# Branch B of a hybrid encoder layer by seven half products, with operand sums held in DRAM

## The chip, the core and the metric

The kernel runs on one core of one Trainium2 chip. The metric is device microseconds of one execution. Three runs of the kernel before gave 1960.22, 1960.53 and 1967.05 us; the median is 1960.53 us.

## The reference

One layer over 2048 tokens of width 1024: a projection to 7168 columns, banded attention (branch A), retention (branch B), both gated and projected, merged, projected again, normalised. What the change touches is the end of it: the gated output of branch B times `w_out_ret`, the merge, and the product with `w_out`.

```python
o_r = retention_chunkwise(qr, kr, v_r.reshape(B, S, R_HEADS, R_VAL_DIM), gn_gain[l])
branch_r = jnp.einsum('bsf,fd->bsd', o_r * jax.nn.silu(g_r), w_out_ret[l])

mixed = jax.nn.sigmoid(m_a) * branch_a + jax.nn.sigmoid(m_r) * branch_r
x = x + jnp.einsum('bsd,de->bse', mixed, w_out[l]).astype(x.dtype)
return rms_norm(x, final_gain)
```

## The kernel before, in words

Everything is float32. Each operand of a large product is split into a high and a low fp32r part, and a product of 128 x 128 weights with 128 x 512 data takes three matmuls: high by high, high by low, low by high. The fixed operand of a stage lies in seven resident pairs of tiles `R[0..6]`, each 128 x 4 x 512; the other operand streams through as chunks of 256 columns, each of them two raw tiles of 512 KB.

A stage is a `Job`. The projections (`p0`, `g0`, `p1`, `g1`) and the last stage (`out`) use the class `Strassen`: a chunk is 2 x 2 halves and is done with seven half products in place of eight, each of 12 matmuls. That needs sums of halves on both sides: `t1` to `t4` of the streaming side are made on POOL (`sum`), and the sums of the resident side stand in `R`. Five PSUM tiles (x, y, v, z, w) are combined by DVE and ACT (`product`).

The output products of branch A (`ba0`, `ba1`) and of branch B (`br0`, `br1`) use the class `Plain`: halves without sums. `ba` has 4 chunks of 4 half products in each half of the tokens, `br` 4 chunks of 8. The number behind a name is the half of the tokens (1024 each). For `br0` and `br1` the eight quarter operands are gated rows: `finish_yr` loads the retention output, its gate and the norm factor (three tiles of 256 KB), multiplies on DVE and POOL and splits into `R`, or, for the first eight, stores to `yrscr` during `p1`, whence `fill_yr` fetches them. `w_out` is loaded and summed during `br1` (`fill_wo`) and split into `R` at its end (`place_wo`).

What sets the order: the program is written by hand. `step()` emits one step of PE work, three matmuls, and then whatever `later(n, ...)` has put n steps ahead. Weights are made three products ahead (`AHEAD`), the high part by ACT (`make`), the low part by DVE four steps later. The engines take this order as written, except that before the change `strict[0]` is off from the opening of the last phase (`mrg`) until the last chunk of `br1`, where a scheduler may reorder ACT, DVE and POOL. Transfers go through SP's queue in the written order; raw chunks of `Strassen` stages go through ACT's queue. Gates (`ga`, `gr`) and earlier results (`ta`) are loaded ahead of each epilogue, and its result is stored (`tas`, `mxs`). SP stops at a store until its data is there.

`p1` starts with two chunks that alternate, product by product (`front=2`, orders `first` and `second`): each pair of `R` is then used twice before the next is needed, while `reload` refills `R`. `out` before starts with one chunk in a special order `s`.

## Time and profile before

| what | us |
|---|---|
| median of three runs | 1960.53 |
| profiled execution, span | 1957.6 |
| PE busy, of the span | 1904.1 (97%) |
| DVE, POOL, ACT busy | 1393.9, 982.5, 936.0 |
| first matmul of `p1`, of its third chunk | 767.46, 810.53 |
| first matmul of `ba0` | 1522.77 |
| first matmul of `br0`, of `out` | 1614.34, 1788.94 |
| last matmul of `out` begins | 1947.44 |

Of the profiled execution the page gives the span; the median of the runs is 2.9 us above it. PE is busy nearly throughout, so the table is read by stages: how many matmuls a stage issues, and how much longer it takes than they need.

### The profile page before, as it was taken

Reading aid. Unit: us, or ns where it says so; the run is one execution under the profiler, and the core shown is the slowest. Engines: PE = TensorE matmul, PEld = TensorE weight load, DVE = VectorE, ACT = ScalarE, POOL = GpSimd, SP = SyncE. Lnnn points to the kernel's source line nnn. Section 1 sums busy time; section 2 is a strip of 40 time slices with the busy share of each in tenths; the row PEclk is TensorE's granted clock in tenths of the full one; section 3 lists DMA queues with packets and bytes.
Section 4 is the critical chain, followed back from the end, with each engine's and each line's share of the span. In section 5 each row is a group of like instructions: output and inputs, shape, how many; then the busy total and the mean of one; then the engine's idle time right before and its main releaser. Section 6 shows DMA issues by size and latency. Waiting matters only on the chain. (4 is left out here: it accounts for less than half of the span.)

```text
span 1957.6 us, 30307 instructions
## 1 busy us (share of the span) xinstructions
PE 1904.1 (97%) x9640; PEld 1589.9 (81%) x9640; DVE 1393.9 (71%) x2551; ACT 936.0 (48%) x1889; POOL 982.5 (50%) x795
## 2 busy tenths in 40 slices
PE   7999999999999999999999999999999999999997
PEld 6887778888888887778787888888888878887886
DVE  6977877677756668888887677765566755547876
ACT  7554564566654555443333555554455321223554
POOL 0543544455546675544544454454666114557775
PEclk9999999999999999999999999999999999999999
DMA  6576786756549987676675645553999899987674
GB/s 191 167 251 205 231 283 206 200 166 178 160 137 278 280 255 266 189 246 188 203 247 170 200 145 163 168 152 116 277 277 297 304 371 330 319 266 234 205 226 140
DMA packets 335054, 434.84 MB, mean 222 GB/s; under 512 B 30040, under 2 KB 194544, under 8 KB 334896
## 3 DMA queue, kind: packets, MB, share of 16 engines
q1 hardware_dynamic: 269152, 368.42, 59.2%
q10 hardware_dynamic: 65744, 64.50, 10.8%
q8 instruction: 77, 1.26, 0.3%
q14 instruction: 81, 0.66, 0.1%
HBM read 288.21 MB, written 144.60 MB: 221 GB/s over the span
## 5 line engine op out<-in xcount | busy, mean ns | idle before, releaser
L142 POOL TENSOR_SCALAR pr<-pr,rsum 128x640 f32<-128x640 f32 (+4 forms) x128 | 96.0, 750 | 226.3 <-DVE ptl L142 108.3
L142 POOL TENSOR_TENSOR t_p<-raw_p,t_p 128x512 f32<-128x512 f32 x50 | 74.0, 1480 | 142.9 <-DVE wl_p L142 129.1
L142 PE MATMUL ps_g_z<-r,wh_g 128*128 128x512 f32 x448 | 143.3, 401 | 2.2 <-DVE c_g L142 2.2
L142 DVE CUSTOM_DVE_ANT_0 pr<-wide,bt 128x640 f32<-128x640 f32 (+4 forms) x128 | 94.3, 737 | 71.6 <-PE wide L142 62.9
L142 PE MATMUL ps_g_x<-r,wh_g 128*128 128x512 f32 x448 | 143.0, 400 | 0.7 <-ACT u_g L142 0.7
L142 ACT ACTIVATE pr<-pr,mn 128x640 f32<-128x640 f32 (+4 forms) x128 | 98.0, 765 | 84.8 <-DVE mn L142 84.8
L142 PE MATMUL ps_p_z<-r,wh_p 128*128 128x512 f32 x416 | 131.5, 397 | 3.1 <-DVE c_p L142 3.1
L142 PE MATMUL ps_p_x<-r,wh_p 128*128 128x512 f32 x416 | 130.1, 394 | 1.5 <-ACT u_p L142 1.5
L142 DVE TENSOR_TENSOR ptl<-tp,pth 128x384 fp32r<-128x384 f32 x168 | 95.9, 573 | 40.7 <-ACT pth L142 40.3
L142 ACT CAST pth<-tp 128x384 fp32r<-128x384 f32 x168 | 84.6, 515 | 70.5 <-PE tp L142 66.7
L142 POOL TENSOR_TENSOR sl<-sm,sh 128x512 fp32r<-128x512 f32 x64 | 88.6, 1384 | 53.9 <-ACT sh L142 26.0
L142 DVE TENSOR_TENSOR wl_p<-t_p,wh_p 128x512 fp32r<-128x512 f32 x104 | 96.8, 932 | 2.1 <-ACT wh_p L142 2.1
L142 DVE TENSOR_TENSOR sm<-sr,dm 128x512 f32<-128x512 f32 x64 | 44.1, 688 | 75.2 <-PE sr L142 37.4
L142 PE MATMUL wide<-ka,qa 128*128 128x512 f32 (+2 forms) x448 | 94.7, 327 | 2.1 <-DVE mn L142 2.1
L142 POOL TENSOR_TENSOR wl_g<-t_g,wh_g 128x512 fp32r<-128x512 f32 x56 | 75.2, 1342 | 41.4 <-ACT wh_g L142 40.2
L142 PEld LDWEIGHTS tp<-ident,pr 128*128 128x128 f32 x560 | 71.3, 141 | 27.4 <-POOL pr L142 2.2
L142 PE MATMUL po<-pth,va 128*128 128x256 f32 x336 | 92.9, 297 | 0.0
L142 PE MATMUL tp<-ident,pr 128*128 128x128 f32 x560 | 89.0, 273 | 2.9 <-POOL pr L142 1.6
L142 PEld LDWEIGHTS wide<-ka,qa 128*128 128x128 f32 x448 | 75.5, 189 | 19.2 <-DVE mn L142 7.3
L142 PEld LDWEIGHTS ps_p_x<-r,wh_p 128*128 128x128 f32 x416 | 76.9, 188 | 17.5 <-ACT u_p L142 2.4
L142 PEld LDWEIGHTS ps_p_z<-r,wh_p 128*128 128x128 f32 x416 | 75.9, 188 | 18.3 <-issue 4.3
L142 PE MATMUL po<-ptl,va 128*128 128x256 f32 x336 | 88.4, 285 | 1.1 <-DVE ptl L142 0.2
(909 smaller groups left out, 6017.9 us busy)
## 6 DMA issues: line engine op xcount, KB each, us to landing
raw_g<-in_w_in_dram ACTq DMA_DIRECT2D x56, 512.0 KB, 5.3
raw_p<-in_w_in_dram ACTq DMA_DIRECT2D x50, 512.0 KB, 6.3
qa<-qas SPq DMA_DIRECT2D x128, 128.0 KB, 2.9
qr<-qrs SPq DMA_DIRECT2D x128, 128.0 KB, 4.3
vr<-vrs SPq DMA_DIRECT2D x64, 256.0 KB, 5.3
ka<-kas SPq DMA_DIRECT2D x40, 256.0 KB, 3.6
va<-vas SPq DMA_DIRECT2D x40, 256.0 KB, 3.1
kds<-kdt_k SPq DMA_DIRECT2D x32, 256.0 KB, 4.1
```

What stands on the lines that cost most here:

```text
L142: return tc.keep_in_program_order(op(*a, **k))
```

## The change

`br0` and `br1` become `Strassen` jobs: seven half products of 12 matmuls a chunk in place of eight. So all seven sums of the gated rows are needed. `piece_yr(s, k)` fetches four gated rows, multiplies them, makes the sums on POOL and DVE and stores seven tiles to `yscr`; it runs four times in `p1` for the first half of the tokens and four times from the opening of `mrg` for the second. `fill_yr` fetches the first half's 28 tiles during `ba0` and `ba1`; `reload` fetches the second half's 28 during the last chunk of `br0` and the first pair of `br1`. `piece_wo` does the same for `w_out` during `p1`, to `wscr`, and `reload` fetches it in the last chunk of `br1` and the first pair of `out`. The first two chunks of `br1` and of `out` alternate as in `p1`; the second chunk's raw quarters are loaded apart (`quarters`). Raw chunks of `br` go through ACT's queue instead of SP's. `strict[0]` stays on. Matmuls in the built program: 9624 before, 9528 now.

```diff
 ORDERS["f"] = LAST = (0, 3, 1, 2, 4, 5, 6)
-ORDERS["s"], ORDERS["o"], ORDERS["l"] = (0, 4, 3, 1, 2, 5, 6), (0, 4, 1, 2, 3, 5, 6), (0, 4, 1, 2, 5, 6, 3)
+ORDERS["b"] = ORDERS["g"]
+ORDERS["o"], ORDERS["l"] = (0, 4, 1, 2, 3, 5, 6), (0, 4, 1, 2, 5, 6, 3)
...
 TR_LATER = 16
-YR_0 = (2, 10, 1)
-YR_1 = (102, 15, 2)
+YR_0 = (12, 90)
+YR_1 = (6, 42)
+WO = (60, 90)
+PAIRED = ("p1", "br1", "out")
...
     orscr = [[D(f"ors_{p}_{b}", [2, P, B]) for b in range(NB)] for p in range(4)]
-    yrscr = [D(f"yrs_{h}", [P, B]) for h in range(HEADS)]
+    yscr = [[D(f"ys_{s}_{m}", [4, P, B]) for m in range(7)] for s in range(2)]
+    wscr = [D(f"ws_{m}", [4, P, B]) for m in range(7)]
...
             if name not in self.ps:
-                two_pools = self.job.name == "out" and name in ("z", "w")
+                two_pools = self.job.name in ("br0", "br1", "out") and name in ("z", "w")
...
         "second": {1: ("t1", "t2"), 2: ("t3",), 5: ("t4",)},
-        "s": {0: ("t1",), 3: ("t2",), 1: ("t3",), 2: ("t4",)},
+        "b": {0: ("t1", "t2"), 2: ("t3",), 6: ("t4",)},
...
             last = self.job.orders[self.c] == "l"
+            lags = (1, 14, 22, 30) if self.c < self.job.front else (1, 4, 7, 10)
             for k, q in enumerate(((1, 1), (1, 0), (0, 1), (0, 0)) if last else ((0, 0), (1, 1), (1, 0), (0, 1))):
-                later(1 + 3 * k, lambda q=q: load(q))
+                later(lags[k], lambda q=q: load(q))
...
             self.orders = [name[0]] * n
-            if name == "g0":
+            if name in ("g0", "br0", "br1"):
...
                 self.orders[front] = "h"
-            if name == "p1":
+            if name in PAIRED:
...
             if name == "out":
-                self.orders[0], self.orders[-1] = "s", "l"
+                self.orders[-1] = "l"
...
             if front:
-                seq[:0] = [(c, n) for n in LAST for c in range(front)] if name == "p1" else [
+                seq[:0] = [(c, n) for n in LAST for c in range(front)] if name in PAIRED else [
...
                 ]
-                if name == "p1":
+                if name in PAIRED:
...
+        for job in jobs:
+            if job.name in PAIRED:
+                one, two_, three = job.chunks[:3]
+                for ch in (one, two_, three):
+                    for lead in RAW_LEADS:
+                        sooner.pop(begins[ch] - lead)
+                two_.raw, three.raw = [], []
+                at = begins[one]
+                sooner[at - 9], sooner[at - 6] = (one, [0]), (one, [1])
...
         later(lag + 2, lambda: (low or dve).tensor_tensor(wl, r32(wl), r32(wh), ALU.subtract))
-    def reload(n):
+    def reload(n, src):
...
             t = 4 * at + k
-            later(1, lambda k=k, t=t: refill(m, k, cscr[m][k], 8 + 2 * t - 4 * at, pool if t % 3 == 2 else dve))
+            later(1, lambda k=k, t=t: refill(m, k, src[m][k], 8 + 2 * t - 4 * at, pool if t % 3 == 2 else dve))
...
+    def piece_yr(s, k):
+        tiles = {}
+        def fetch(i, j):
+            h, b = 4 * j + k, 2 * s + i
+            a, u, r = (E(f"{n}_{h}_{b}") for n in ("yr", "yv", "rb"))
+            tiles[i, j] = a
+            dma(a, orscr[h // 2][b][h % 2])
+            dma(u, urscr[h][b])
+            dma(r, rsscr[s][8 * b + h].rearrange("(o d) -> o d", o=1).broadcast_to([P, B]))
+            later(14, lambda: dve.scalar_tensor_tensor(a, a, gn[:, h:h + 1], u, ALU.mult, ALU.mult))
+            later(16, lambda: pool.tensor_tensor(a, a, r, ALU.mult))
+        def store(m, t, lag):
+            put(lag + 4, yscr[s][m][k], t)
+        def first():
+            s1 = tiles["s1"] = E(f"ys1_{s}_{k}")
+            pool.tensor_tensor(s1, tiles[1, 0], tiles[1, 1], ALU.add)
+            store(2, tiles[1, 1], 0)
+            store(3, s1, 3)
+        def second():
+            a11 = tiles[0, 0]
+            s2 = tiles["s2"] = E(f"ys2_{s}_{k}")
+            dve.tensor_tensor(s2, tiles["s1"], a11, ALU.subtract)
+            dve.tensor_tensor(tiles[1, 0], tiles[1, 0], a11, ALU.subtract)
+            store(0, a11, 0)
+            store(4, s2, 2)
+            store(5, tiles[1, 0], 2)
+        def third():
+            a12 = tiles[0, 1]
+            s4 = E(f"ys4_{s}_{k}")
+            pool.tensor_tensor(s4, a12, tiles["s2"], ALU.subtract)
+            store(1, a12, 0)
+            store(6, s4, 3)
+        for n, q in enumerate(((1, 0), (1, 1), (0, 0), (0, 1))):
+            later(1 + 3 * n, lambda q=q: fetch(*q))
+        later(23, first)
+        later(27, second)
+        later(30, third)
+    def fill_yr(n):
+        m = PRODUCTS[n][0]
         for k in range(4):
-            later(1 + 2 * k, lambda k=k: refill(m, k, yrscr[4 * j + k], 10))
+            later(1 + 2 * k, lambda k=k: refill(m, k, yscr[0][m][k], 10))
+    def quarters(ch, src):
+        ch.b = {}
+        for key in ("b11", "b12", "b21", "b22"):
+            ch.b[key] = E(f"{key}_{ch.job.name}", shape=(P, 4, P))
+            h = int(key[2]) - 1
+            dma(ch.b[key], src(int(key[1]) - 1)[:, :, h * P:(h + 1) * P])
...
             d, b = 2 * c + j, 2 * s + i
-            g, ta = C(f"gr_{d}_{b}"), C(f"ta_{d}_{b}")
+            g, ta = E(f"gr_{d}_{b}"), E(f"ta_{d}_{b}")
...
     def ep_br(s):
-        def epilogue(c, i, j, ps, got):
-            g, ta = got
-            dve.scalar_tensor_tensor(g, g, 1.0, ps, ALU.add, ALU.mult)
-            pool.tensor_tensor(g, g, ta, ALU.add)
+        def epilogue(c, i, j, src, ps):
+            g, ta = by_name[f"br{s}"].chunks[c].got.pop((i, j))
+            dve.scalar_tensor_tensor(g, g, 1.0, src, ALU.add, ALU.mult)
+            later(1, lambda: pool.tensor_tensor(g, g, ta, ALU.add))
...
         return epilogue
-    wo = {}
-    def fill_wo(k):
+    def piece_wo(k):
...
         s2, s3, s4 = (E(f"ws{n}_{k}") for n in (2, 3, 4))
-        wo[4, k], wo[5, k], wo[2, k], wo[6, k] = s2, s3, a[1, 1], s4
...
+        def store(lag, m, t):
+            put(lag, wscr[m][k], t)
...
             dve.tensor_tensor(s2, s3, a[1, 1], ALU.add)
+            pool.tensor_tensor(a[1, 0], a[1, 0], a[1, 1], ALU.add)
+            for n, (m, t) in enumerate(((0, a[0, 0]), (2, a[1, 1]), (5, s3), (4, s2), (3, a[1, 0]))):
+                store(2 + n, m, t)
...
+            store(5, 1, a[0, 1])
+            store(6, 6, s4)
...
     ]
-    RYA = [{(0, 0): 0, (1, 0): 4}, {(0, 0): 5, (1, 0): 2}]
-    RYR = [{(0, 0): 6, (0, 1): 1, (1, 0): 3, (1, 1): 0}, {(0, 0): 4, (0, 1): 5, (1, 0): 2, (1, 1): 6}]
+    RYA = [{(0, 0): 0, (1, 0): 4}, {(0, 0): 2, (1, 0): 6}]
...
         jobs.append(Job(f"br{s}", 4, w_stream(w_out_ret, [T * c for c in range(4)]), ep_br(s),
-                        resident=RYR[s], before=before_br(s)))
-    jobs.append(Job("out", 8, mx_stream, ep_out, (2, 5), before=before_out))
+                        before=before_br(s), front=2 * s))
+    jobs.append(Job("out", 8, mx_stream, ep_out, (2, 5), before=before_out, front=2))
+    by_name = {j.name: j for j in jobs}
...
     for n in range(7):
-        hook("g0", 13, n, lambda n=n: reload(n))
+        hook("g0", 13, n, lambda n=n: reload(n, cscr))
+        hook("br0", 3, n, lambda n=n: reload(n, yscr[1]))
+        hook("br1", 3, n, lambda n=n: reload(n, wscr))
...
     hook("g1", 13, 1, lambda: fill_ya(0, 1, 4))
-    for j in range(2):
-        hook("g1", 13, 6, lambda j=j: later(66 * j, lambda: fill_yr(j, RYR[0][0, j])))
...
         hook("ba0", 1 + i, 0, lambda i=i: fill_ya(1, i, RYA[1][i, 0]))
-    for k in range(4):
-        hook("br1", *divmod(1 + 6 * k, 8), lambda k=k: fill_wo(k))
-    hook("br1", 3, 2, lambda: strict.__setitem__(0, True))
-    for n, m in ((4, 4), (5, 5), (6, 2), (7, 6)):
-        hook("br1", 3, n, lambda n=n, m=m: place_wo(m, *((1, 1) if n < 6 else (n - 4, 2))))
+    for at, n in ((("ba0", 0, 1), 2), (("ba0", 2, 0), 3), (("ba0", 3, 0), 4), (("ba1", 0, 0), 0),
+                  (("ba1", 1, 0), 1), (("ba1", 3, 2), 5), (("ba1", 3, 3), 6)):
+        hook(*at, lambda n=n: fill_yr(n))
+    br1, out_job = by_name["br1"], by_name["out"]
+    hook("br0", 2, 4, lambda: quarters(br1.chunks[1], lambda j: br1.stream(1, j)))
+    hook("br1", 2, 4, lambda: quarters(out_job.chunks[1], lambda j: out_job.stream(1, j)))
...
     seq.extend((job, ch, n) for job in jobs for ch, n in job.seq)
-    for j in (jobs[0], jobs[2]):
-        for i in range(2):
-            hook(j.name, i, 1 if j is jobs[2] else (0, 1, 1), lambda j=j, i=i: j.chunks[2].load([i]))
+    for j in jobs:
+        for i in range(2 if j.front else 0):
+            hook(j.name, i, 1 if j.name in PAIRED else (0, 1, 1), lambda j=j, i=i: j.chunks[2].load([i]))
...
+    quarters(jobs[2].chunks[1], lambda j: jobs[2].stream(1, j))
     run_to(end["g0"])
-    for h in range(HEADS):
-        later(10 + 44 * h, lambda h=h: finish_yr(h, 0, None, 18))
+    for k in range(4):
+        later(YR_0[0] + YR_0[1] * k, lambda k=k: piece_yr(0, k))
+        later(WO[0] + WO[1] * k, lambda k=k: piece_wo(k))
...
     st.close()
-    strict[0] = False
     st = open_phase("mrg", E_MRG, 4)
-    free_at = end["br0"] - 12
...
+    for k in range(4):
+        later(YR_1[0] + YR_1[1] * k, lambda k=k: piece_yr(1, k))
...
```

SP's queue, where `ba1` ends and `br0` begins. `ga` and `gr` are gates on their way in, `ta` branch A's result, `tas` its store, `yr`, `yv`, `rb` the three inputs of a gated row, `r` a tile of `R`, `ys` the stored sums. Before:

```order
L142 DMA ga_7_2_18465<-mas_7_2_364 128x512
L142 DMA tas_6_2_424<-ga_6_2_18420 128x512
L142 DMA ga_7_3_18487<-mas_7_3_365 128x512
L142 DMA tas_6_3_425<-ga_6_3_18443 128x512
L142 DMA gr_0_0_18505<-mrs_0_0_366 128x512
L142 DMA ta_0_0_18506<-tas_0_0_398 128x512
L142 DMA tas_7_2_428<-ga_7_2_18465 128x512
```

Now, from the same load on:

```order
L145 DMA ga_7_2_18731<-mas_7_2_377 128x512
L145 DMA tas_6_2_437<-ga_6_2_18685 128x512
L145 DMA ga_7_3_18756<-mas_7_3_378 128x512
L145 DMA gr_0_0_18762<-mrs_0_0_379 128x512
L145 DMA ta_0_0_18763<-tas_0_0_411 128x512
L145 DMA yr_2_3_18769<-ors_1_3_317 128x512
L145 DMA yv_2_3_18770<-urs_2_3_289 128x512
L145 DMA rb_2_3_18771<-rss_1_453 128x512
L145 DMA tas_6_3_438<-ga_6_3_18709 128x512
L145 DMA gr_1_1_18784<-mrs_1_1_384 128x512
L145 DMA ta_1_1_18785<-tas_1_1_416 128x512
L145 DMA r21_86<-ys_0_2_328 128x512
```

Between the load of `ga_7_2` and the store of its product stood five transfers; now it is seventeen, of which the eleven rows under the first are shown.

ACT's queue, where `out` begins. `wh_out_c_n` is the high part of chunk c's weights for product n, `r40` the high part of `R[4]`, `ws2` a sum of `w_out` in SBUF, `r01` the raw tile that a refill has put in the low half. Before:

```order
L142 CAST r40_89<-ws2_0_19320 128x512
L142 CAST wh_out_0_0_19900<-raw_out_0_0_19804 128x512
L142 CAST r40_89<-ws2_1_19453 128x512
L142 CAST r40_89<-ws2_2_19586 128x512
L142 CAST r40_89<-ws2_3_19719 128x512
L142 CAST r50_91<-ws3_0_19321 128x512
L142 DMA raw_out_1_0_19928<-mxs_0_430 128x4x256
L142 CAST wh_out_0_4_19930<-t1_out_0_19865 128x512
```

Now:

```order
L145 CAST r00_81<-r01_82 128x512 x2
L145 CAST wh_out_0_0_20288<-raw_out_0_0_20122 128x512
L145 CAST r00_81<-r01_82 128x512
L145 CAST r10_83<-r11_84 128x512
L145 CAST wh_out_0_3_20317<-raw_out_0_1_20206 128x512
L145 CAST r10_83<-r11_84 128x512 x2
L145 CAST wh_out_1_0_20349<-b11_out_20112 128x512
L145 CAST r10_83<-r11_84 128x512
L145 CAST r40_89<-r41_90 128x512
L145 CAST wh_out_1_3_20377<-b21_out_20116 128x512
```

The weights of two chunks now come in turn, and every cast into `R` follows a transfer instead of a tile that lies in SBUF.

More of the change, by code (lines that the diff above doesn't have):

```diff
@@ L503, in dense @@
         sooner = {at - lead: (ch, [j]) for ch, at in begins.items() for j, lead in enumerate(RAW_LEADS)}
-        one, two_, three = jobs[2].chunks[:3]
-        for ch in (one, two_, three):
-            for lead in RAW_LEADS:
-                sooner.pop(begins[ch] - lead)
-        two_.raw, three.raw = [], []
-        at = begins[one]
-        sooner[at - 9], sooner[at - 6] = (one, [0]), (one, [1])
-        first_out = jobs[-1].chunks[0]
-        at = begins[first_out]
-        for lead in RAW_LEADS:
-            sooner.pop(at - lead)
-        sooner[at - 8], sooner[at - 5] = (first_out, [0]), (first_out, [1])
+        for job in jobs:
[7 more added lines that the diff above has]
+                sooner[at - 9], sooner[at - 6] = (one, [0]), (one, [1])
         operands = {begins[ch] - 2: ch for ch in begins if ch.job.before}
@@ L1101, in fill_ya @@
             later(1 + k, lambda k=k: refill(m, k, oascr[k][2 * s + i], 8))
-    def finish_yr(h, b, m, lead, hold=0):
-        a, u, r = (E(f"{n}_{h}_{b}") for n in ("yr", "yv", "rb"))
-        dma(a, orscr[h // 2][b][h % 2])
-        dma(u, urscr[h][b])
-        dma(r, rsscr[b // 2][8 * b + h].rearrange("(o d) -> o d", o=1).broadcast_to([P, B]))
-        def gated():
-            dve.scalar_tensor_tensor(a, a, gn[:, h:h + 1], u, ALU.mult, ALU.mult)
-        later(lead, gated)
-        later(lead + 2, lambda: pool.tensor_tensor(a, a, r, ALU.mult))
-        if m is None:
-            put(lead + 8, yrscr[h], a)
-            return
-        wh, wl = (w[:, h % 4, :] for w in R[m])
-        at = max(lead + 5, hold - steps[0])
-        later(at, lambda: act.copy(wh, a))
-        later(at + 2, lambda: dve.tensor_tensor(wl, a, r32(wh), ALU.subtract))
@@ L1819, in hybrid_kernel @@
     st.close()
-    strict[0] = False
     st = open_phase("mrg", E_MRG, 4)
-    free_at = end["br0"] - 12
-    for s, (first, every, of) in enumerate((YR_0, YR_1)):
-        for n, (i, h) in enumerate((i, h) for i in range(1 - s, 2) for h in range(HEADS)):
-            hold = free_at + h % 4 if s and i and h > 3 else 0
-            later(
-                first + every * n // of,
-                lambda s=s, i=i, h=h, hold=hold: finish_yr(h, 2 * s + i, RYR[s][i, h // 4], 8, hold),
-            )
+    for k in range(4):
+        later(YR_1[0] + YR_1[1] * k, lambda k=k: piece_yr(1, k))
     while step():
```

21 lines of the change are left out of this document (removed).

## The prediction

> **What bounds the kernel now.** The page's first line says that PE is busy almost throughout, so I read PE's own waits from branch A's output products to the end, then the stretches of that part, then the instants at which stages begin.
>
> ```profile
> PE 1904.1 (97%) x9640; PEld 1589.9 (81%) x9640; DVE 1393.9 (71%) x2551; ACT 936.0 (48%) x1889; POOL 982.5 (50%) x795
> PE ps_out_x L142 <- ACT u_out L142: 3.4, 1, 3.4
> PE ps_out_z L142 <- DVE c_out L142: 0.7, 1, 0.7
> ```
> ```profile
> core 0: us, PE busy (x) PEld busy (x) DVE busy (x) ACT busy (x) POOL busy (x), PEclk, DMA share, GB/s
> 1553.00:1614.30 61.30, 61.18 (x266) 49.32 (x265) 35.56 (x56) 14.78 (x25) 10.31 (x8) 1.00 1.00 363
> 1614.30:1701.40 87.10, 87.10 (x385) 72.11 (x385) 47.76 (x65) 18.51 (x33) 41.16 (x29) 1.00 0.96 332
> 1701.40:1788.90 87.50, 87.31 (x385) 72.03 (x384) 45.63 (x55) 20.46 (x37) 47.75 (x34) 1.00 0.76 251
> 1788.90:1814.40 25.50, 21.42 (x86) 16.69 (x86) 22.66 (x21) 11.03 (x23) 22.26 (x14) 0.93 0.76 244
> ```
>
> The second and third line are two of three waits of PE after 1523 us (the third is 0.2 us). In the table the first row is the end of branch A's products, the next two are `br0` and `br1`, the last is the first chunk of `out`. PE is the bound of branch B: no wait, full clock. Beside it the column before the last shows something nearly as full: the DMA engines, 1.00 and 0.96 of their time.
>
> **The change part by part.**
>
> ```profile
> 1614.34 0.61 PE L142 MATMUL ps_br_(0, 0)_18528<-r,wh_br_(0, 0)_18462 128*128 128x512 f32 x2
> 1788.94 0.61 PE L142 MATMUL ps_out_x<-r,wh_out 128*128 128x512 f32 x2
> 1814.39 0.62 PE L142 MATMUL ps_out_x<-r,wh_out 128*128 128x512 f32 x2
> 1833.43 0.62 PE L142 MATMUL ps_out_x<-r,wh_out 128*128 128x512 f32 x2
> ```
>
> *Products.* These rows open `br0`, `out`, and the second and third chunk of `out`. A chunk of seven products is 84 matmuls and takes 1833.43 - 1814.39 = 19.04 us without a wait, 0.2267 us each (2.72 us a product; a step of the program is three, 0.68 us). Branch B takes 1788.94 - 1614.34 = 174.6 us for 768 matmuls. 672 take 152.3 us: **-22.3 us**. Nothing hides this, since PE is the bound.
>
> *Start of `out`.* Its first chunk takes 1814.39 - 1788.94 = 25.45 us, 6.4 more than the next. `place_wo` then fills ACT and DVE with splits of `w_out`, and one wait does most of the harm:
>
> ```profile
> 1797.91 0.90 PE L142 MATMUL ps_out_x<-r,wh_out 128*128 128x512 f32 x2 [3.37 <-ACT u_out L142]
> 1798.00:1802.00 4.00, 4.00 (x11) 3.13 (x12) 4.00 (x4) 2.46 (x5) 4.00 (x4) 0.57 0.98 367
> ```
>
> PE waits 3.37 us for the copy of a product, and in the 4 us behind it the granted clock is 0.57. The alternating start replaces this chunk: **-6.4 us**, but it has a price of its own, which `p1` shows, since it starts in the same way.
>
> ```profile
> 767.46 0.61 PE L142 MATMUL ps_p_x<-r,wh_p 128*128 128x512 f32 x2
> 810.53 0.61 PE L142 MATMUL ps_p_x<-r,wh_p 128*128 128x512 f32 x2
> 767.50:810.50 43.00, 39.53 (x169) 31.12 (x168) 42.81 (x46) 24.19 (x46) 30.15 (x18) 1.00 0.65 226
> 810.50:1058.90 248.40, 243.91 (x1124) 200.04 (x1123) 204.66 (x276) 92.90 (x178) 110.65 (x75) 1.00 0.68 219
> 1059.51 0.71 PE L142 MATMUL ps_g_x<-r,wh_g 128*128 128x512 f32 x2
> ```
>
> The first two rows open `p1` and its third chunk, the last opens the stage behind `p1`.
>
> Two chunks take 810.53 - 767.46 = 43.07 us where 168 matmuls need 38.08: 5.0 us lost, with DVE busy 42.81 of 43.00. `br1` and `out` each do the same on DVE (28 refills, of which POOL takes nine, 14 low parts, the combinations of two chunks): twice 5.0, **+10.0 us**, between 4 (`br1` and `out` have two more PSUM tiles a chunk from the second pool) and 14.
>
> *More work in `p1`.* `piece_yr` and `piece_wo` bring 32 operations to DVE and 32 to POOL where `finish_yr` had eight and eight.
>
> ```profile
> L142 DVE SCALAR_TENSOR_TENSOR yr<-yr,gn,yv 128x512 f32<-128x512 f32 x7 | 5.2, 744 | 0.0
> L142 DVE TENSOR_TENSOR wl_p<-t_p,wh_p 128x512 fp32r<-128x512 f32 x48 | 45.6, 950 | 0.0
> L142 DVE TENSOR_TENSOR c_p<-ps_p_z,u_p 128x512 f32<-128x512 f32 x13 | 9.0, 690 | 0.4
> L142 POOL TENSOR_TENSOR t_p<-raw_p,t_p 128x512 f32<-128x512 f32 x23 | 33.5, 1457 | 70.8 <-DVE wl_p L142 62.1 <-DMA raw_p<-in_w_in_dram 6.4 <-POOL t_p L142 2.0
> L142 POOL TENSOR_TENSOR yr<-yr,rb 128x512 f32<-128x512 f32 x7 | 11.6, 1664 | 6.4 <-DVE yr L142 6.4
> ```
>
> 24 more at 0.744 to 0.950 us are 18 to 23 us of DVE, 24 at 1.457 to 1.664 are 35 to 40 us of POOL. In `p1` behind its first pair DVE is busy 204.66 of 248.40 us, so the work fits on average (some 90%), but DVE works in order and every low part of a weight passes through it. If a fifth of DVE's addition comes at a bad moment, **+4 us**; the bounds are 0 (all of it in DVE's idle time) and 10 (half of it on the path). The transfers, 88 more, take about 60 us of the DMA engines in 291 us, where the share is 0.65 to 0.68: covered.
>
> *Branch B's other engines.* POOL gets 32 sums, some 47 us at 1.457 us, in 152 us where it was busy 89 of 175 and loses half of the gated rows: it has room. DVE in `br0` gets 28 low parts (26.6 us), 20 combinations and 16 epilogues at 0.69 us (25 us), and about 22 us of refills and gated rows, 73 of 76 us. I cost this at nothing only because the next term makes PE wait at the same place; without that wait it may cost 0 to 5 us.
>
> *Transfers.* Here is the term that decides. In the trace the DMA engines are full for 30 us, at this rate and these landing times:
>
> ```profile
> DMA packets 7092, 11.64 MB, mean 388 GB/s; under 512 B 662, under 2 KB 2173, under 8 KB 7090
> ga<-mas SPq DMA_DIRECT2D x11, 256.0 KB, 5.3
> r<-yrs SPq DMA_DIRECT2D x4, 256.0 KB, 6.3
> out_dram<-fg SPq DMA_DIRECT2D x30, 256.0 KB, 2.2
> ```
>
> The first three lines are from 1560 to 1590 us, the last is the median of the stores in `out`, where little else moves. From 1553 us to the end of `br0` the kernel now moves 363 GB/s x 61.3 us + 332 x 87.1 = 51.2 MB in 148.4 us. In the built order the same stretch has 181 transfers before and 227 after: 21 loads of gated rows fewer, but 32 more fills of `R`, 28 stores of sums, and some single ones. 46 more of 0.262 MB make 63.3 MB. At 388 GB/s that is 163.1 us, and PE will need only 61.3 + 76.2 = 137.5 us: 25.6 us of transfers too many. Most come from the 20th us of the stretch on, when a piece's 12 loads and 7 stores join the gates and the fills.
>
> How much of it stays unnoticed? A gate of branch A is loaded two products (5.4 us) ahead of its epilogue, and the low parts that stand behind that epilogue on DVE are due eight steps (5.4 us) later. A fill's cast stands ten steps (6.8 us) behind its transfer, and the weights behind it on ACT are due 12 steps (8.2 us) later. Less the 2.2 us of an easy landing, a backlog of 8.7 to 12.8 us does no harm. So PE waits 12.8 to 16.9 us. I take the low end, **+13 us**, because the worst backlog stands where the fills for `br0` do. The bounds are 0 and the whole 25.6. That `br`'s raw chunks go through ACT's queue frees SP, not the engines: in the 30 us above SP's queue alone had them full.
>
> The Trainium skill, "DMA: Bandwidth & Descriptors", section Specifications, puts the limit of a core towards HBM at about 358 GB/s and that of the ports at 435. The trace's 388 lies between them and decides. By 358 the surplus would be an estimated 39 us and the change slower; by 435 it would be an estimated 8 us, within what does no harm, which is the first rival below.
>
> **Sum:** -22.3 - 6.4 + 10.0 + 4 + 13 = -1.7 us, a span of 1955.9. The median of the runs is 2.9 us over the profiled span (1960.53 to 1957.6), so **1958.8 us**: no change. What a measurement of this kernel can tell from no change is about 0.5%, 9.8 us: faster means below 1950.7, slower above 1970.3.
>
> **The rivals.**
>
> *The transfers hide.* If the backlog never exceeds what is tolerated (loads issued with their buffers free, stores that can wait, engines that move more than 388 GB/s when the mix has more stores), the 13 us go: -14.7 us, **1945.8**. For it: the existing queue is full for 60 us (share 1.00) and PE does not wait once. Against it: the surplus is twice the tolerated backlog.
>
> *SP's queue becomes the bound.* SP takes its transfers in order and stops at a store until its data is there. Seventeen transfers instead of five then lie between a gate and the store of its product, twelve more at 0.68 us each, 8 us. If a late gate stops the store, and the stop keeps loads back that would have filled the engines, nothing of the surplus is hidden. PE then waits 25.6 us in several pieces, some above the 3.37 us at which the granted clock fell to 0.57; three such pieces at 1.7 us (the 4 us at 0.57) add 5. With 7 us in `p1` the sum is -22.3 - 6.4 + 10 + 7 + 25.6 + 5 = +19, **1979**. It decides from about 21 us of waiting on, since -28.7 + 10 + 7 + 21.5 is the 9.8 of a slower kernel. The Trainium skill, "TensorE: Matmul & The Clock Gate", Part 1, has the clock fall after an idle window of about 3.4 us and return after as long a busy one; the trace agrees here (3.37 us), and by it waits well below cost no clock.
>
> *The change does not give what it says*: the sums cost PE elsewhere as much as the products gave, by DVE in `p1` and branch B (10 + 5 us) and both starts (14): -28.7 + 29, **1961** with the transfers hidden.
>
> **How the numbers follow.** The forecast has 0.42, the hidden transfers 0.32, SP's queue 0.23, the last 0.03. Faster by over 0.5% is the second case, 0.32; slower the third, 0.23; within 0.5% the first and last, 0.45. The range reaches to both rivals' times, 1942 to 1979: about half of the slow one lies above it and a quarter of the hidden one below (0.11 + 0.08). The likeliest case alone runs from 1952 to 1969 (DMA term from 8 to 20, `p1` and starts as bounded).
>
> **What the profile after would show.** 12 matmuls fewer per chunk of branch B: its first to last matmul without waits 152.3 us. The start of `out` to its third chunk 43 us, with waits for DVE. In the list of PE's waits from 1553 us to the end of `br0`: behind them ACT's casts into `R` and DVE's epilogues that wait for DMA, the DMA share at 1.0 for all of `br0`, landing times of gates and fills above 12 us. If these land in 6 us, the transfer term is wrong; if `p1` (292.1 us from 767.46 to 1059.51) grows by over 10 us, that term is; if PE waits for DVE alone, it is the third rival.

## The result, and the profile after

The changed kernel takes 2047.54 us (median of 4 runs, 2044.40 to 2051.89) against 1960.82 us of the kernel before (4 runs): a ratio of 1.0437, 95% interval 1.0419 to 1.0454. It is slower by 87 us, where no change was forecast.

The page, then the rows of PE that open `p1`, its third chunk, `g1`, `br0`, `br1`, `out` and `out`'s third and fourth chunk:

```profile
PE 1914.0 (94%) x9544; PEld 1581.6 (77%) x9544; DVE 1528.0 (75%) x2645; ACT 967.2 (47%) x1945; POOL 1087.8 (53%) x853
```
```profile
767.31 0.61 PE L145 MATMUL ps_p_x<-r,wh_p 128*128 128x512 f32 x2
...
820.08 0.39 PE L145 MATMUL ps_p_x<-r,wh_p 128*128 128x512 f32 x1
...
1092.97 0.48 PE L145 MATMUL ps_g_x<-r,wh_g 128*128 128x512 f32 x1
...
1676.96 0.39 PE L145 MATMUL ps_br_x<-r,wh_br 128*128 128x512 f32 x1
...
1775.84 0.39 PE L145 MATMUL ps_br_x<-r,wh_br 128*128 128x512 f32 x1
...
1866.31 0.39 PE L145 MATMUL ps_out_x<-r,wh_out 128*128 128x512 f32 x1
...
1917.67 0.39 PE L145 MATMUL ps_out_x<-r,wh_out 128*128 128x512 f32 x1
...
1939.67 0.39 PE L145 MATMUL ps_out_x<-r,wh_out 128*128 128x512 f32 x1
```

There are 96 matmuls fewer, and DVE is busy 134 us longer. From one opening to the next (the same rows taken in both traces, `ba0` opening at 1522.77 and 1557.91, and the experiments below read likewise):

| stage | before | after | change | of it products alone |
|---|---|---|---|---|
| p1, first two chunks (the pair) | 43.1 | 52.8 | +9.7 | 38.1 |
| p1, the rest | 249.0 | 272.9 | +23.9 | 228.5 |
| ba0 + ba1 | 91.6 | 119.0 | +27.5 | |
| br0 | 87.1 | 98.9 | +11.8 | 76.2 |
| br1 | 87.5 | 90.5 | +3.0 | 76.2 |
| out, first two chunks | 44.5 | 51.4 | +6.9 | 38.1 |
| out, the rest | 114.0 | 117.0 | +3.0 | |

`g1` with attention and retention in it grows by 1.6 us; together 87 us. Now each engine in these stages (the columns are those of the prediction's tables):

```profile
767.30:820.10 52.80, 43.95 (x170) 33.88 (x169) 52.52 (x53) 24.98 (x47) 39.44 (x24) 0.90 0.78 266
820.10:1093.00 272.90, 251.59 (x1130) 203.10 (x1128) 231.37 (x295) 93.04 (x177) 141.47 (x95) 0.98 0.81 268
1557.90:1610.50 52.60, 47.25 (x217) 38.33 (x215) 32.73 (x52) 16.87 (x31) 5.75 (x5) 0.99 0.96 326
1610.50:1677.00 66.50, 52.00 (x193) 39.82 (x194) 38.10 (x48) 13.17 (x23) 19.53 (x14) 0.85 0.92 323
1677.00:1775.80 98.80, 82.36 (x337) 64.82 (x336) 80.03 (x85) 26.64 (x47) 65.40 (x42) 0.95 0.97 327
1775.80:1866.30 90.50, 81.13 (x337) 63.37 (x336) 83.57 (x85) 34.83 (x63) 67.40 (x43) 0.98 0.79 276
1866.30:1917.70 51.40, 41.53 (x170) 32.10 (x169) 49.91 (x44) 21.80 (x44) 44.98 (x28) 0.97 0.68 234
```

Two things stand out at once. In `ba` and `br0` (rows three to five) the DMA engines are nearly full (share 0.92 to 0.97) at 323 to 327 GB/s, not 388. In both pairs DVE is full, and in `br1` nearly so; its 85 operations there take 83.57 us, almost 1 us each. Why is seen beside POOL, first DVE's rows of the timeline in `br1`, then POOL's:

```profile
1783.67 1.77 DVE L145 TENSOR_TENSOR wl_br<-b_br,wh_br 128x512 fp32r<-128x512 f32 x1
1785.36 1.77 DVE L145 TENSOR_TENSOR r<-r,r 128x512 fp32r<-128x512 f32 x1
1787.05 1.77 DVE L145 TENSOR_TENSOR wl_br<-b_br,wh_br 128x512 fp32r<-128x512 f32 x1
1788.75 1.75 DVE L145 TENSOR_TENSOR r<-r,r 128x512 fp32r<-128x512 f32 x1
1790.43 0.68 DVE L145 SCALAR_TENSOR_TENSOR gr<-gr,ps_br_x 128x512 f32<-128x512 f32 x1
```
```profile
1784.85 1.73 POOL L145 TENSOR_TENSOR t_br<-b_br,b_br 128x512 f32<-128x512 f32 x1
1786.66 1.62 POOL L145 TENSOR_TENSOR t_br<-b_br,t_br 128x512 f32<-128x512 f32 x1
1788.24 1.71 POOL L145 TENSOR_TENSOR r<-r,r 128x512 fp32r<-128x512 f32 x1
1789.92 1.73 POOL L145 TENSOR_TENSOR t_br<-raw_br,raw_br 128x512 f32<-128x512 f32 x1
```

The two engines go in step, one operation of each every 1.7 us, and the only short one of DVE's reads an operand from PSUM (`ps_br_x`). The experiments test what that means. In `ba` SP's waits show a third thing. Behind them stand the transfer of ACT that the longest of them was for, and SP's transfers just before and after that wait:

```profile
SPq L145 <- DMA raw_br<-in_w_out_ret_dram: 15.8, 3, 5.8
```
```profile
1637.23 0.38 ACTq L145 DMA_DIRECT2D raw_br<-in_w_out_ret_dram  x1
```
```profile
1639.03 0.32 SPq L145 DMA_DIRECT2D rb<-rss  x1
1645.16 0.32 SPq L145 DMA_DIRECT2D r<-ys  x1
```

The program gives each transfer the next of eight semaphores in turn and lets it wait until the transfer eight before it has landed, whichever engine issued that. ACT issued the weight chunk `raw_br` late, behind casts that waited for their data, and SP, with a fill of `R` ready to go, stood 5.8 us until it had landed.

The fourth is the granted clock (the column PEclk). It falls to half at twelve places between the openings of `p1` and of `out`'s third chunk, where the kernel before has one. Here is one of them in `br0`, with the matmuls of PE and the windows of the fall and of what follows:

```profile
1738.77 0.50 PE L145 MATMUL ps_br_x<-r,wl_br 128*128 128x512 f32 x1 [1.83 <-DVE wl_br L145]
...
1739.95 1.05 PE L145 MATMUL ps_br_x<-r,wh_br 128*128 128x512 f32 x2
```
```profile
1739.60:1743.00 3.40, 3.40 (x10) 2.62 (x9) 3.40 (x4) 0.00 (x0) 2.77 (x3) 0.50 0.93 246
1743.00:1746.40 3.40, 3.40 (x15) 2.50 (x14) 3.40 (x4) 1.76 (x3) 3.40 (x3) 1.00 1.06 405
```

A wait of 1.83 us comes before 3.4 us at half clock, in which PE does ten matmuls instead of 15 (two of them in 1.05 us, where 0.61 is usual). So a wait can cost more than its own length: in `p1` PE is idle 22 us more than before and its matmuls take some 10 us longer.

### The profile page after: what moved, and what is told of

Same layout as the page of the kernel before. It is cut to its first block, busy times and chain, and to the rows that moved or that the text cites. A ratio compares the mean times of both kernels' runs of the same rounds, so it can differ in the third digit from the quotient of the medians.

```text
span 2045.1 us, 30651 instructions
## 1 busy us (share of the span) xinstructions
PE 1914.0 (94%) x9544; PEld 1581.6 (77%) x9544; DVE 1528.0 (75%) x2645; ACT 967.2 (47%) x1945; POOL 1087.8 (53%) x853
## 4 chain that ended last, share of the span: by engine, by line
PE 33%; DMA 12%; DVE 12%; issue 6%; POOL 4%; ACT 1%; SPq 1%; POOLq 0%; DVEq 0%; ACTq 0%
PE ps_g_z L145 4%; PE ps_g_x L145 4%; PE o L145 2%; PE po L145 2%; PE ps_g_v L145 2%; PE ps_g_y L145 2%; PE ps_g_w L145 2%; DMA raw_br<-in_w_out_ret_dram 2%; PE wide L145 2%; DVE r L145 2%; DMA r<-ys 2%; DVE wl_p L145 1%; POOL fg L145 1%; DMA yv<-urs 1%; PE tp L145 1%
## 5 line engine op out<-in xcount | busy, mean ns | idle before, releaser
L145 DVE CUSTOM_DVE_ANT_0 pr<-wide,bt 128x640 f32<-128x640 f32 (+4 forms) x128 | 94.3, 737 | 71.5 <-PE wide L145 63.3
L145 DVE TENSOR_TENSOR r<-r,r 128x512 fp32r<-128x512 f32 x101 | 107.4, 1075 | 11.3 <-ACT r L145 11.3
L145 ACT CAST r<-r 128x512 fp32r<-128x512 f32 x128 | 76.1, 618 | 71.5 <-DMA r<-ys 52.6
L145 POOL TENSOR_TENSOR yr<-yr,rb 128x512 f32<-128x512 f32 x32 | 47.7, 1492 | 108.4 <-DVE yr L145 103.0
L145 DVE TENSOR_TENSOR sm<-sr,dm 128x512 f32<-128x512 f32 x64 | 44.1, 689 | 79.8 <-PE sr L145 38.1
L145 DVE TENSOR_TENSOR wl_p<-t_p,wh_p 128x512 fp32r<-128x512 f32 x104 | 101.3, 975 | 1.7 <-ACT wh_p L145 1.7
L145 ACT CAST wh_p<-t_p 128x512 fp32r<-128x512 f32 x104 | 64.4, 619 | 60.5 <-DVE wl_p L145 21.5
L145 PEld LDWEIGHTS tp<-ident,pr 128*128 128x128 f32 x560 | 71.3, 140 | 27.5 <-POOL pr L145 2.2
```

The costliest lines, as they stand in the source:

```text
L145: return tc.keep_in_program_order(op(*a, **k))
```

## The experiments

A stage that an experiment leaves alone differs from one profiled execution to the next: `p1` takes 322.6 to 328.7 us, `ba0` to `br0` 217.9 to 223.2, `br0` 98.5 to 104.0, `br1` 88.4 to 90.5, `out`'s pair 51.4 to 52.4. A stage's change counts only if it leaves that range. The changed kernel's ratio is 1.0437 (1.0419 to 1.0454) throughout. The intervals of e1, e3, e4, e5, e6, e9, e10 and e15 overlap with it, so what these show is read from their stages.

**What the seven products cost alone (e8).**

```diff
-        hook("br0", 3, n, lambda n=n: reload(n, yscr[1]))
-        hook("br1", 3, n, lambda n=n: reload(n, wscr))
...
-            dma(ta, tascr[d][b])
...
-            later(1, lambda: pool.tensor_tensor(g, g, ta, ALU.add))
...
-        later(YR_1[0] + YR_1[1] * k, lambda k=k: piece_yr(1, k))
```

> Branch B's seven products stay, but what goes with them in br0 and br1 is left out: batch 1's pieces, the refills of R in br0's and br1's last chunks, and branch A's term (its loads and additions), so the output is not the reference's. If the products are as cheap as counted and DVE, POOL and the transfers eat the gain: br0 76 to 82 us, br1 76 to 79, the pair of out 38 to 41, ba0+ba1 105 or less. Rival, something in the seven products themselves (PSUM banks, the order of the chunks) holds PE up: br0 and br1 stay above 85.

The windows of `ba0`, `ba1`, `br0`, `br1` and `out`'s pair:

```profile
1561.70:1609.20 47.50, 46.92 (x218) 38.54 (x217) 32.05 (x53) 19.85 (x36) 5.64 (x4) 1.00 0.91 310
1609.20:1652.80 43.60, 43.60 (x194) 35.96 (x193) 25.91 (x37) 11.56 (x21) 4.45 (x3) 1.00 0.96 336
1652.80:1730.30 77.50, 76.75 (x338) 62.94 (x337) 49.27 (x71) 24.07 (x41) 28.66 (x21) 1.00 0.59 199
1730.30:1809.30 79.00, 76.97 (x337) 62.79 (x336) 44.27 (x65) 19.39 (x32) 16.96 (x13) 1.00 0.50 166
1809.30:1849.40 40.10, 38.75 (x170) 31.41 (x170) 23.58 (x28) 13.35 (x28) 22.08 (x17) 1.00 0.59 180
```

Ratio 1.0061 (1.0037 to 1.0084), with `p1` as long as in the changed kernel. Nearly all as counted, and `ba` is back at 91.1 us although it still fills `R` from DRAM. What eats the gain is what goes with the products, not the products; which part of it, e8 can't say, since it leaves out pieces, refills and branch A's term together.

**POOL and DVE (e3, e4, e5).** e3 leaves POOL's additions of branch A's term out, e4 and e5 move operations from POOL to DVE.

```diff
e3  -            later(1, lambda: pool.tensor_tensor(g, g, ta, ALU.add))
e4  -  refill(m, k, src[m][k], 8 + 2 * t - 4 * at, pool if t % 3 == 2 else dve)
    +  refill(m, k, src[m][k], 8 + 2 * t - 4 * at, dve)
e5  -            later(16, lambda: pool.tensor_tensor(a, a, r, ALU.mult))
    +            later(16, lambda: (pool if s else dve).tensor_tensor(a, a, r, ALU.mult))
    (likewise s1, s4 and the two of piece_wo)
```

> The addition of branch A's term to branch B's (POOL, 32 times 1.65 us in br0 and br1) is left out, its loads stay, so the output lacks branch A. Theory that POOL's operations hold up DVE's on SBUF operands: DVE's busy time falls by 0.7 to 1.0 us for each that is gone although DVE loses none of its own instructions, some 10 to 15 us in each of br0 and br1; br1, 90.5 us with 76.2 of products, falls to 80 to 84, br0 from 98.9 to about 92. Rival, DVE is full by its own instructions and POOL is a free helper: br0 and br1 unchanged within 2 us. Rival, transfers set br0: br0 unchanged.

> The nine of 28 low parts of R that POOL works out at each stage change (to p1, br1 and out) go to DVE. Shared way: an operation of POOL takes DVE as long as or longer than the same operation on DVE (0.684 us alone), so the pairs of p1 (52.8 us), br1 and out (51.4) change by -4 to +1 us each, and the run by -10 to +2. Rival, POOL's work is free for DVE: nine times 0.68 us more on a full engine, 5 to 6 us longer for each pair, 15 to 18 in all.

> In p1 the 32 operations of the pieces that POOL does go to DVE; nothing else changes. Shared-way theory: in a stretch where DVE is full, an operation on POOL costs DVE about 1.05 us (1.73 of the two side by side less DVE's own 0.68) and the same on DVE 0.684, so p1 (52.8 + 272.9 us) gets 5 to 12 us shorter. Rival, POOL works beside DVE for nothing: DVE gets 22 us more and p1 is 10 to 20 us longer.

`br0` and `br1` in e3:

```profile
1679.40:1780.50 101.10, 84.42 (x338) 66.76 (x337) 70.95 (x86) 28.46 (x51) 46.74 (x32) 0.92 0.97 338
1780.50:1863.90 83.40, 78.66 (x338) 62.76 (x336) 67.58 (x84) 33.74 (x60) 37.76 (x25) 1.00 0.82 293
```

In `br1` POOL has 18 operations fewer and DVE, with its own instructions unchanged, is busy 16.0 us less, 0.89 us for each; the stage falls from 90.5 to 83.4 us and `out`'s pair from 51.4 to 45.9. `br0` gains nothing from DVE's relief (101.1 us, where some 92 were expected): something else ends last there. The ratio is 1.0412 (1.0383 to 1.0442). e4: the pairs of `p1` and `out` 49.0 and 48.2 us (-3.8, -3.2), `br1` unchanged, ratio 1.0410 (1.0383 to 1.0436). e5: `p1` 318.5 us (-7.2), ratio 1.0413 (1.0394 to 1.0432), with these windows of `p1`:

```profile
771.40:820.90 49.50, 41.04 (x169) 32.12 (x168) 49.31 (x56) 23.72 (x45) 27.66 (x17) 0.97 0.77 268
820.90:1089.90 269.00, 251.06 (x1130) 201.61 (x1129) 232.19 (x324) 93.90 (x179) 103.76 (x69) 0.99 0.82 274
```

DVE does 32 operations more, and it is busy 281.5 us instead of 283.9. Work moved from POOL to a full DVE makes the stage shorter: the rival, a free helper, fails each time.

**p1 (e2, e6, e10, e15).** e2 takes the pieces' arithmetic out but no transfer and no buffer; e6 moves the pieces out of the pair; e10 and e15 put their arithmetic earlier or later.

```diff
e2   -            dve.tensor_tensor(s2, tiles["s1"], a11, ALU.subtract)
     +            act.copy(s2, a11)
     (likewise s1, s4 and w_out's three; gating, row factors and in-place sums left out)
e6   -YR_0 = (12, 90)          +YR_0 = (60, 80)
     -WO = (60, 90)            +WO = (100, 80)
e10  14, 16 | 23, 27, 30 | lag + 4   ->   10, 11 | 16, 20, 23 | lag + 1
e15  14, 16 | 23, 27, 30             ->   22, 24 | 31, 35, 38
```

> In p1 the pieces of the gated rows (batch 0) and of w_out keep every load, store and buffer, but their arithmetic on DVE and POOL is left out, and ACT copies stand in for the sums, so the output is not the reference's. DVE theory: p1 grew by 33.5 us (325.7 against 292.1) because DVE, full in the pair and nearly so behind it, got 28 operations more and was held up by 28 of POOL's; p1 falls to 300 us or below. Rival, a shortage of E buffers and SP's queue behind it (in chunk 4 DVE waited 7.96 us for a vat buffer): p1 stays above 318. If both hold, p1 lies between, some 308.

> The four pieces of gated rows start at steps 60, 140, 220, 300 of p1 instead of 12, 102, 192, 282, those of w_out at 100, 180, 260, 340, so none falls into the pair of alternating chunks (56 steps). DVE theory, place: the pair goes from 52.8 us back to 43 to 45, and since the rest of p1 has DVE idle only some 12 of 273 us, part of the gain comes back there: p1 3 to 9 us shorter in all. Rival, the place does not matter (the total of DVE's work sets p1): p1 within 2 us of 325.7. Rival, E buffers: without a piece in the pair the wait in the fifth chunk goes too, over 12 us.

> In p1 a piece of gated rows does its arithmetic 4 to 7 steps sooner after its loads and stores its sums 3 steps sooner, so that its 15 E buffers come free some 5 to 7 us earlier; the instructions are the same. Ring theory (p1's fifth chunk, 30.4 instead of 20.9 us, in which DVE was idle for 7.96 us for a buffer of kds): that chunk falls to 21 to 25 us and p1 (325.7) by 8 to 15. DVE theory: no change in sum, within 3 us, since DVE and POOL have the same to do. Risk to both: a load that has not landed stops DVE at the piece, p1 some us longer.

> In p1 a piece of gated rows does its arithmetic 8 steps (5.4 us) later after its loads, the opposite of e10. Theory that DVE, which works in order, stops at the gating for loads that have not landed (12.8 us of DVE's idle time in p1 are waits for yv and yr): these waits go and p1 (325.7) gets 5 to 12 us shorter. Ring theory (E buffers held 5.4 us longer keep the projections' own buffers back): the waits for ACT's vat (9.9 us) grow and p1 is 3 to 10 us longer. Only DVE's amount of work counts: within 3 us.

e2's windows of `p1`:

```profile
765.30:807.60 42.30, 39.31 (x169) 31.15 (x168) 42.11 (x46) 25.58 (x49) 28.43 (x17) 1.00 0.89 311
807.60:1055.20 247.60, 244.27 (x1130) 200.53 (x1129) 193.08 (x270) 104.36 (x200) 100.72 (x69) 1.00 0.88 299
```

That is 289.9 us for `p1`, below the 292.1 of before (ratio 1.0267, 1.0229 to 1.0305), and the granted clock stays at 1.00. All of the growth is arithmetic; the 88 added transfers and the buffers cost nothing by themselves. e6: the pair is back at 42.0, the rest grows from 272.9 to 280.5; the whole, 322.5, is 3.2 us shorter, hardly outside the range (ratio 1.0430). e10: 323.3 (ratio 1.0454); the fifth chunk falls from 30.4 to 27.2, and the eighth rises from 21.2 to 28.9. e15: 322.3 (ratio 1.0443); DVE's longest waits in `p1`, two without and two with that edit:

```profile
DVE yr L145 <- DMA yv<-urs: 11.1, 5, 4.6
DVE vat L145 <- ACT vat L145: 9.9, 3, 8.0
```
```profile
DVE vat L145 <- ACT vat L145: 10.0, 4, 7.1
DVE u_p L145 <- PE ps_p_w L145: 6.7, 5, 2.8
```

The stops for gated rows are gone, and `p1` is 3.4 us shorter, again hardly outside the range. So neither a stop for loads nor the ring of E buffers is the cause of most of it; wherever the pieces stand, about the same is lost.

**ba and br0 (e1, e7, e9).** e1 puts all loads of weights on one queue, e7 moves fewer bytes (the product takes the gate in place of the row factor), e9 moves the second and third piece of `mrg`.

```diff
e1  -  (dma if self.job.resident else act.dma_start)(raw, ...)
    +  (dma if self.job.resident or self.job.name in ("br0", "br1") else act.dma_start)(raw, ...)
e7  -            dma(r, rsscr[s][8 * b + h]...)
    +            if s == 0:
    +                dma(r, rsscr[s][8 * b + h]...)
e9  -        later(YR_1[0] + YR_1[1] * k, lambda k=k: piece_yr(1, k))
    +    for k, at in enumerate((6, 36, 68, 132)):
    +        later(at, lambda k=k: piece_yr(1, k))
```

> The weight chunks of branch B's two stages are issued from SP's queue, as before the change, instead of ACT's. Queue theory: at most eight transfers are on the way at a time, and in the trace SP stood 15.8 us in ba0 and ba1 and 20.1 us in br0 for a raw_br that ACT had issued late; with one queue that goes, ba0+ba1 (119.1 us in the profile after, 90.1 before the change's 29 us) lose 15 us or more and the run is some 15 to 25 us shorter, about 2025 us. Rival, DMA engines simply full: the same bytes take the same time, under 3 us. Rival, DVE and POOL share a way into SBUF: no change in ba, br0 within 3 us.

> The 16 broadcast loads of batch 1's row factors are left out (the product takes the gate in their place, so the output is not the reference's): 4.2 MB of 61.6 MB between the start of ba1 and the end of br0, every operation stays. Theory that transfers bound ba and br0 (after: 52.6 + 66.4 + 98.9 = 217.9 us, DMA share 0.92 to 0.97): 8 to 12 us shorter. Theory that SP's order with the late weight loads of ACT is all: under 4 us. Theory that DVE bounds br0: br0 unchanged, ba 0 to 3 us shorter.

> Batch 1's four pieces start at steps 6, 36, 68 and 132 of the last phase instead of 6, 48, 90 and 132, so that the third no longer loads while br0 starts; in the trace that start has SP issuing a transfer every 0.68 us for 20 us, the fills for br0's first chunk late and that chunk at 33.1 us instead of 19. Place theory (only a local heap of transfers): br0's first chunk falls to 22 to 27 us, ba1 grows by less than 4, a gain of 5 to 10 us in ba0 to br0 (217.9). Capacity theory (the bytes of the whole stretch set its length): ba1 grows by what br0 gains, the sum stays within 3 us.

e1: `ba0`, `ba1`, `br0` 53.0, 59.7, 96.3 us, together 209.0 against 217.9; ratio 1.0411 (1.0389 to 1.0433). SP's wait for `raw_br` is gone from `ba`. That is the queue's share, 8.9 us against the changed kernel's execution; `ba` lost 6.4 us, where 15 or more were expected. What is left runs at full DMA engines, here in `ba1`:

```profile
1606.60:1666.30 59.70, 51.64 (x192) 39.83 (x193) 39.25 (x49) 13.14 (x22) 20.03 (x14) 0.89 1.00 355
```

e7: `ba0` to `br0` 211.0 us, a gain of 6.9 us for 4.2 MB (12 us at 342 GB/s, the rate worked out below), in `ba` alone, a little under what was expected; ratio 1.0393 (1.0370 to 1.0416). e9: `br0` -1.4, `ba1` +3.4, sum +2.3, ratio 1.0446. Moving transfers about gains nothing, as the capacity theory has it, and `br0`'s first chunk stays at 32.2 us.

**All together (e12, e13), and the lesson on the kernel before (e11, e14).** e12 is e1, e4, e5 and the edit below; e13 has the sums on DVE as well. e11 and e14 start from the kernel before.

```diff
e12  -            later(1, lambda: pool.tensor_tensor(g, g, ta, ALU.add))
     +            later(1, lambda: dve.tensor_tensor(g, g, ta, ALU.add))
e13  -            pool.tensor_tensor(b[dst], b[one], b[two], ALU.subtract)
     +            eng = dve if self.job.name in ("br0", "br1") or self.job.name in PAIRED and self.c < 2 else pool
     +            eng.tensor_tensor(b[dst], b[one], b[two], ALU.subtract)
e11  reload: pool if t % 3 == 2 else dve -> dve;  finish_yr, m is None: pool -> dve
e14  e11, and sum: pool -> dve for p1's first two chunks and out's first;  place_wo: pool -> dve
```

> Four edits together: branch B's weight chunks on SP's queue (e1: -8.4 us in ba0 to br0), the refills' low parts all on DVE (e4: -3.8 and -3.2 us in the pairs of p1 and out), p1's pieces without POOL (e5: -7.2), and branch A's term added by DVE instead of POOL (32 operations; new). If the causes are separate, the first three give 22 to 23 us, about 2024; the new one, by the shared way 0.37 us for each that falls where DVE is full, 0 to 6 us more in br1 and the pair of out. Rival, the causes overlap (what is freed in one place waits in the next): under 12 us in all. Either way the run stays slower than the kernel before, since the transfers of ba0 to br0 and the arithmetic of p1 remain.

> As e12, and the sums of weight quarters in br0, br1 and the pairs of p1 and out on DVE too, so that POOL does next to nothing there. Shared-way theory: br1 (90.5 us after), with 126 operations of DVE at 0.684 us, comes to 84 to 88 and the pairs to 44 to 48, a further 3 to 10 us. Rival, DVE in its order is too late for the sums that POOL did ahead: no gain or a loss against e12.

> The kernel before the change, with the nine low parts of p1's refills and the eight products of finish_yr in p1 moved from POOL to DVE. Shared-way theory: p1's pair, 43.1 us with DVE full, gets 1 to 3.5 us shorter, p1 (292.1) 2 to 5, the run 0.1 to 0.3% faster. Rival: POOL is a free helper, p1 3 to 8 us longer.

> The kernel before the change with e11's edits, and further POOL's sums of weight quarters in p1's pair and out's first chunk and its part of w_out's last splits on DVE. Shared-way theory: p1's pair (43.1; 41.0 in e11) 39 to 41 us, out's first chunk (25.5) 21 to 24, the run 0.2 to 0.5% under the kernel before. Rival, DVE in its order comes too late for the sums that POOL works out ahead: out's first chunk 26 us or more and no gain.

e12: 2017.01 us, ratio 1.0277 (1.0256 to 1.0297), 0.0160 or 31 us under the changed kernel, above the 22 to 29 expected. By stages it is 6.7 us in `p1`, 9.9 in `ba0` to `br0`, 3.9 in `br1` and 5.4 in `out`'s pair. So the causes in different stages stand beside each other; in `p1` the 3.8 of e4 and the 7.2 of e5 don't add in full. e13: 2011.40 us, 1.0247 (1.0214 to 1.0280), not told apart from e12 by the run's time; the pair of `p1` 47.0, `br1` 80.0 and the pair of `out` 44.4 us. `br1`'s window in e13, and three of DVE's groups in it; behind them the same groups of the changed kernel (the number after the comma is the mean in ns):

```profile
1755.70:1835.70 80.00, 77.67 (x337) 62.88 (x336) 75.66 (x124) 33.91 (x60) 0.00 (x0) 1.00 0.80 285
```
```profile
L145 DVE TENSOR_TENSOR r<-r,r 128x512 fp32r<-128x512 f32 x28 | 18.9, 680 | 0.0
...
L145 DVE TENSOR_TENSOR wl_br<-t_br,wh_br 128x512 fp32r<-128x512 f32 x16 | 10.9, 681 | 0.0
...
L145 DVE TENSOR_TENSOR c_br<-ps_br_z,u_br 128x512 f32<-128x512 f32 x4 | 2.7, 685 | 0.9 <-PE ps_br_z L145 0.8
```
```profile
L145 DVE TENSOR_TENSOR r<-r,r 128x512 fp32r<-128x512 f32 x20 | 26.6, 1332 | 0.0
L145 DVE TENSOR_TENSOR wl_br<-t_br,wh_br 128x512 fp32r<-128x512 f32 x16 | 22.1, 1385 | 0.1
...
L145 DVE TENSOR_TENSOR c_br<-ps_br_z,u_br 128x512 f32<-128x512 f32 x4 | 2.7, 686 | 2.2 <-PE ps_br_z L145 2.2
```

With POOL idle, DVE does 124 operations in less time than the changed kernel's 85, those of two SBUF tiles at 0.68 us each; that with a PSUM operand takes the same in both.

e11: 0.9992 (0.9980 to 1.0004), no difference that can be told; `p1`'s pair 41.0 and `p1` 289.2 us. e14: 0.9968 (0.9954 to 0.9981), 1958.34 against 1964.77 us on the same chip. This beats the kernel before by 0.3%. But `p1` is 289.6 us, no shorter than in e11, and `out`'s first chunk stays at 25.9, where the rival held; in which stage the rest of the gain arises isn't shown.

## Why the prediction was wrong

*Products, -22.3.* Right but for 4 us: without what goes with them `br0` and `br1` take 77.5 and 79.1 us (e8), 18.0 us under before, 1.3 and 2.9 us over the products.

*Operations on DVE and POOL.* This step failed first. The prediction charged DVE with its own additions and POOL with POOL's, as if neither slowed the other, and said of POOL in branch B that it has room. In `p1` it took a fifth of DVE's addition as delay, +4, at most +10; `p1` grew by 33.5, more than three times the bound. From the windows, DVE's busy time in `p1` grows from 42.81 + 204.66 to 52.52 + 231.37, by 36.4 us: 24 operations at 0.684 (an expectation said 28) are 16.4; the other 20.0, if all of them are DVE held up by POOL's 24, are 0.83 us each. The 18 to 23 us that the prediction gave DVE were little more than half of what it got. It even quoted low parts at 950 ns on the mean, where e13's take 681: held-up ones were among them. That the pieces' arithmetic on a DVE that is 87% busy (283.9 of 325.7 us) lengthens `p1` is shown by e2, and by e5 that POOL's part of it costs more than the same on DVE. By which waits it does so stays open, with e10 and e15, and the exchange isn't one for one: DVE's time and `p1` fall by 48.7 and 35.8 us in e2, by 2.4 and 7.2 in e5.

The Trainium skill, "SBUF — State Buffer", section "SBUF: two separate sides", says that DVE and POOL share a pair of ports to SBUF, that an operation of DVE with two SBUF inputs and one of POOL that reads SBUF hold it for their whole length, and that the other one waits. The traces agree: 1.77 us beside POOL, 0.68 with a PSUM operand or with POOL idle. By it POOL's 24 operations would have been charged to DVE as well.

*Starts, +10.0 and -6.4.* `p1`'s pair as the measure of a start was right in kind, but that one had 18 of POOL's operations in it and `out`'s has 28. `out`'s pair takes 51.4 instead of 43.1, `br1`'s first two chunks 27.3 + 24.1 = 51.4: each lost 13.3 us, not 5.0. With less of POOL (12 operations) the pair of `out` takes 44.4 (e13), and without refills 40.0 (e8). So the alternating start of `out` takes 6.9 us more than the start that it replaced, where 1.4 less was forecast.

*Transfers, +13.* The mechanism, a backlog of transfers that PE waits for, was right; the size was wrong, by the rate and by what a wait does to the clock. From 1588 us (the 1553 of before) to the end of `br0` the kernel moves

```profile
1588.00:1775.80 187.80, 151.51 (x601) 117.82 (x601) 131.59 (x153) 45.12 (x79) 86.84 (x57) 0.92 0.96 328
```

187.8 x 328 = 61.6 MB, near the 63.3 forecast. But 388 GB/s was the best stretch of the trace; full engines gave 363 / 1.00 and 332 / 0.96 = 346 in rows that the prediction quoted, and 328 / 0.96 = 342 here. At 342 the 63.3 MB take 185 us, not 163.1: a surplus of 48 us, which less the tolerated 8.7 to 12.8 makes PE wait 35 to 39. The stretch takes 187.8 - 137.5 = 50.3 us more than PE needs. Of these PE is idle for 187.8 - 151.5 = 36.3, of which e1's single queue takes away 9 to 10. The other 15 are matmuls at a lower clock: 601 at 0.2267 us would be 136.2, and they take 151.5, at a granted clock of 0.92. That the rate sets the rest of the idle time fits e7 and e9 but is argued, not shown. The prediction had worked out the case of the Trainium skill's 358 GB/s ("DMA: Bandwidth & Descriptors", section Specifications) and set it aside for the trace's 388; the mean of this stretch lies below both.

*The clock* was put at nothing in the forecast and at 5 us in the second rival, on the reading that waits well below 3.4 us cost none. The trace after doesn't bear that out: 1.83 us of waiting came before half clock. It cost about 15 us from `ba1` to the end of `br0` and 10 in `p1`, where PE's busy time grows from 283.4 us (x1293) to 295.5 (x1300). With the waits gone, it is 1.00 throughout `p1` (e2).

*ACT's queue for the weights* was said to free SP. It ties SP to ACT instead: 15.8 us of SP's waits in `ba`, 8.9 us of the time (e1). This is the second rival's stop, by another door than its late gates: for the products of `ga` that its stores need, SP waits only 14.3 us from `ba0` to the end of `br0`, less than for the late chunks (35.9) and less than before (22.2).

*DVE in `br0`, 0 to 5*, can't be told from the transfers: with 9 us less of DVE's time (e3) `br0` got no shorter.

*What the profile after was to show.* "If these land in 6 us, the transfer term is wrong" was a wrong test. They land in 5 us, where over 12 were forecast, by the list of issues from 1600 to 1677 us:

```profile
ga<-mas SPq DMA_DIRECT2D x20, 256.0 KB, 5.2
...
r<-ys SPq DMA_DIRECT2D x12, 256.0 KB, 5.1
```

With eight on the way, 8 x 0.262 MB are 5.4 us at 388 GB/s and 6.1 at 342; a backlog stands ahead of the issue, in SP's queue, and is not seen in landing times. The other test (`p1` over 10 us longer) named the failed term.

*The rivals.* The third, sums that cost PE elsewhere what the products gave, which had a chance of 0.03, came true at twice its price: `p1` and both starts lost 33.5 + 13.3 + 13.3 = 60 us, against the 29 that it named. The transfers, which it took for hidden, came on top, and a stop of SP's beside them. What is left in e13, 2011 us, is `p1` (+20 us against before) and `ba` with `br0` (+35 us), that is the pieces' arithmetic and the transfers, with the clock that their waits cost.

## What to carry to other kernels

Work put on POOL beside a busy DVE is not free: price an operation of POOL on SBUF tiles of this size (128x512, float32) at some 0.8 to 0.9 us of DVE's time, and where DVE is full move it to DVE, which took 0.68. Size a bound by transfers with the rate of full engines over the whole stretch, not with its best 30 us, and look for the backlog ahead of the issue instead of in landing times. When transfers are given to a second engine's queue, see which semaphores both share: a late issue there can stop the first.

## What was not expected of the hardware

- DVE's 128x512 operation of two SBUF tiles takes 0.68 us with POOL idle and 1.77 beside POOL's, one with a PSUM operand 0.68 in both.
- Full DMA engines moved between 342 (328 at a share of 0.96) and 388 GB/s, according to the stretch.
- A wait of PE of 1.83 us came before 3.4 us at half of the granted clock.
